# One core, one transformer layer in f32 by split products: w_ffn_out by Strassen's scheme as well

## The chip, the cores and the metric

One core of a Trainium2 chip runs the whole layer. The metric is the device time of one execution in microseconds (us). Five engines work side by side: PE (TensorE, matrix products; PEld is its loading of weights), DVE (VectorE), ACT (ScalarE), POOL (GpSimd) and SP (SyncE, which here only issues transfers).

## The reference

A batch of one, 512 tokens, width 1024, one layer. The first half mixes tokens in four branches (a short convolution, a gated spatial mixing, and two kinds of attention), gates them and multiplies by `w_out`. The second half, in which the change lies, is a gated feed-forward block with 2816 hidden rows:

```
h = h + mixer(rms_norm(h, norm_mix_g))
h = h + swiglu(rms_norm(h, norm_ffn_g), w_ffn_in, w_ffn_out)

def _swiglu(x, w_in, w_out):
    g, u = jnp.split(x @ w_in, 2, axis=-1)
    return (jax.nn.silu(g) * u) @ w_out
```

All inputs and the output are f32.

## The kernel before, in words

Everything is held transposed: features on the 128 partitions, the 512 tokens along the free axis. A matrix of weights is cut into blocks of 128 x 128. So that PE can run its faster f32 form without losing precision, each operand is split in two parts, `hi` (ACT copies it to the rounded type, line 180) and `lo` (DVE subtracts, line 181), and a product is three matmuls: hi hi, hi lo, lo hi (`mm3`, lines 200 to 202, all through line 187). Weights come in chunks of eight blocks, 128 x 1024 f32 or 512 KB, in the order of use (`STREAM`); SP loads a chunk into `raw`, and ACT and DVE split it into `whi` and `wlo`, of which there are three each.

The feed-forward stage has 22 row tiles of hidden rows (each 128). Rows 0 to 3 (`PLAIN`) are computed by `mm3` with 512 columns while the operands for Strassen's scheme are formed. Rows 4 to 21 go in pairs by Strassen's scheme in Winograd's form (`quad_rows`): the tokens are cut into halves of 256, the 1024 inputs into halves of 512, and for a pair of row tiles the gate side and the up side are the other dimension's halves. Seven products (named by their operands 11, s1, s2, 12, s3, 22, s4) take the place of eight; each has 8 blocks x 3 = 24 matmuls of 256 columns (`product`, lines 890 to 892). The four weight blocks of a pair, each 128 x 1024, are loaded by SP (`quad_pair`, line 873) into four pairs of `sraw` tiles; DVE forms their four sums (lines 913, 915, 922, 927), and ACT and DVE split each product's weights. `quad_begin` starts the next pair's first product ahead of the last two of this one. DVE and ACT combine the products (lines 896, 920, 921, 926, 933, 935, 938), and the pair's hidden rows are split at once into `xg` tiles.

`w_ffn_out` is multiplied in three groups of 8, 8 and 6 rows (`GROUPS`): after the rows of a group, `column` computes for each of the eight output tiles the products with the group's hidden rows, 512 columns each, and DVE adds the sum to the residual `h1[d]` (line 962). In the last group the first two columns begin with four of the six rows, and one of them is put into the last pair; each finished tile is sent out.

A planner (Tile) puts every engine's instructions in an order that it works out ahead of time by a simulated timeline, and sets the waits. The order of the program is a priority to it and not a law, except for PE's instructions in the plain rows (`pinned`). A pool of tiles can be closed and its memory used by a later one (`mix.close()`); tiles of one tag share a number of buffers.

Of the kernel before, what the change touches and what calls it, by code (L numbers as in the profile page):

```python
# [29 lines left out]

PLAIN = 4
GROUPS = (8, 8, 6)

PAIRS = 4
# [20 lines left out]
def unit_stream():  # L55

    s = []

    def block(m, col, ks):
        for k in ks:  # L60
            s.append((m, k, col))

    for k in range(KT):
        for nm in ("sbq", "sbk"):
            for b in range(2):
                s.append(("w_in", k, OFF[nm] + b * P))
# [10 lines left out]
    for first, n in hidden_groups():  # L77
        if not first:
            for j in range(PLAIN):
                block("w_ffn_in", j * P, range(KT))  # L80
                block("w_ffn_in", FFN + j * P, range(KT))
        for d, js, _ in out_steps(first, n):
            block("w_ffn_out", d * P, js)
    return s


def out_steps(first, n):


    rows = range(first, first + n)  # L90
    if first + n < FK:
        return [(d, rows, True) for d in range(KT)]
    return [(0, rows[:-2], False), (1, rows[:-2], False), (0, rows[-2:], True), (1, rows[-2:], True)] + \
        [(d, rows, True) for d in range(2, KT)]
# [13 lines left out]
def hidden_groups():  # L108
    first = 0
    for n in GROUPS:  # L110
        yield first, n
        first += n
    assert first == FK


def quad_stream():

    return [(j, half, side) for j in range(PLAIN, FK, 2) for half, side in ((0, 0), (0, 1), (1, 1), (1, 0))]  # L120
# [3 lines left out]
NCHUNK = -(-len(STREAM) // UNITS)  # L124
# [3 lines left out]
def mixer_kernel(ctx, tc, xT, units, quads, wt1, wt2, wsT, small, out):  # L128
# [6 lines left out]
    sm = ctx.enter_context(tc.tile_pool(name="sm", bufs=4))  # L135
    psum = ctx.enter_context(tc.tile_pool(name="psum", bufs=1, space=bass.MemoryType.PSUM))

    mix = ExitStack()
    slots = mix.enter_context(tc.tile_pool(name="slots", bufs=1))

    BUFS = dict(y=18, att=4, aug=6, mrg=8, tmp=6, gt=4)
    KEEP = ("mrg", "tmp", "gt")
# [6 lines left out]
    def slot(tag, dtype=F32):  # L149
        return (keep if tag in KEEP else slots).tile([P, T], dtype, tag=tag, bufs=BUFS[tag], name=nm(tag))  # L150
# [56 lines left out]
    def load_units(c, part, parts):  # L207
        if part == 0:
            chunks[c] = (wpool.tile([P, UNITS * P], F32, tag="raw", bufs=3, name=nm("raw")),
# [32 lines left out]
    sml = const.tile([P, N_SMALL], F32, name="sml")  # L242
# [7 lines left out]
    ssum = slot("mrg")  # L250
# [22 lines left out]
    ident_r = const.tile([P, P], F32R, name="ident_r")  # L273
# [6 lines left out]
    tri = const.tile([P, P], F32, name="tri")  # L280
# [3 lines left out]
    ntri = const.tile([P, P], F32, name="ntri")  # L284
    negs = const.tile([P, P], F32, name="negs")
# [3 lines left out]
    ntri_r = const.tile([P, P], F32R, name="ntri_r")  # L289
    V.tensor_copy(ntri_r, ntri)  # L290
    negs_r = const.tile([P, P], F32R, name="negs_r")
# [5 lines left out]
    mask_sb = const.tile([P, P], F32R, name="mask_sb")  # L297
# [4 lines left out]
    mask_fx = const.tile([P, P], F32R, name="mask_fx")  # L302
# [8 lines left out]
    hm_r = const.tile([P, P], F32R, name="hm_r")  # L311
# [41 lines left out]
    nc.sync.dma_start(out=sml, in_=small)  # L353
    rc, r1 = rms(ssum, "r1")
# [12 lines left out]
    u = []  # L367
    for b in range(2):
        t = slot("mrg")
# [4 lines left out]
    def token_group(wt, width, nk, banks):  # L374

        for c in range(KT // nk):
            raw = wpool.tile([P, nk * width], F32, tag="raw", bufs=3, name=nm("raw"))
# [59 lines left out]
    gq = const.tile([P, 1], F32, name="gq")  # L437
# [283 lines left out]
    def gates(n):  # L721
        gate = {}
        for kind, d in gate_steps(n):
# [9 lines left out]
            if n == 0:  # L733
                merged[d] = slot("mrg")
# [14 lines left out]
    h1, hg = [], []  # L749
    hsum = slot("tmp")  # L750
    tab = const.tile([P, 1], F32, name="tab")
    for d in range(KT):
# [5 lines left out]
        hd = slot("mrg")  # L758
        V.tensor_tensor(hd, ps, x_d, op=ALU.add)
        g = sml[:, C_G2 + d:C_G2 + d + 1]  # L760
# [14 lines left out]

    mix.close()
    ffn = ctx.enter_context(tc.tile_pool(name="ffn", bufs=1, reuse_waits="tile"))
    H = T // 2

# [3 lines left out]
    def plain_product(row, col, ks, ps):  # L783
        for k in ks:
            mm3(ps, next_unit(("w_ffn_in", k, col)), hg[k], k == 0, k == KT - 1)

    def plain_gate(ps):
        t = slot("gt")
# [5 lines left out]
    def plain_up(j, t):  # L794
        up = bank("g") if j else up0
        plain_product(j, FFN + j * P, range(0 if j else 2, KT), up)
# [10 lines left out]
    plain_product(0, 0, range(6), gp)  # L807
    _, r2 = rms(hsum, "r2", lambda: (plain_product(0, 0, range(6, KT), gp), plain_product(0, FFN, range(2), up0)))
# [9 lines left out]

    A = [ffn.tile([P, 2, 4, H], F32, tag="sraw", bufs=PAIRS, name=nm("A")) for _ in range(2)]

    def normed(half):
        for k in range(4):
            d = 4 * half + k
            g = sml[:, C_G2 + d:C_G2 + d + 1]
            V.scalar_tensor_tensor(A[half][:, :, k], h1[d].rearrange("p (h t) -> p h t", h=2), g,
                                   r2.rearrange("p (h t) -> p h t", h=2), op0=ALU.mult, op1=ALU.mult)

    def operand(src):
        hi, lo = (ffn.tile([P, 4, H], F32R, tag="op", bufs=14, name=nm("op")) for _ in range(2))
        split(hi, lo, src)  # L830
        return hi, lo

    a11, a21, a12, a22 = A[0][:, 0], A[0][:, 1], A[1][:, 0], A[1][:, 1]
    X = {}

    def operands(step):
        if step == 0:
            normed(0)
            X["11"] = operand(a11)
        elif step == 1:  # L840
            normed(1)
            X["22"] = operand(a22)
            V.tensor_tensor(a22, a21, a22, op=ALU.subtract)
            X["s1"] = operand(a22)
        elif step == 2:
            V.tensor_tensor(a21, a11, a21, op=ALU.subtract)
            V.tensor_tensor(a11, a22, a11, op=ALU.subtract)
            X["s2"] = operand(a11)
            X["12"] = operand(a12)
        elif step == 3:  # L850
            X["s3"] = operand(a21)
            V.tensor_tensor(a12, a12, a11, op=ALU.add)
            X["s4"] = operand(a12)

    t = plain_gate(gp)
    for j in range(PLAIN):
        if j:
            gp = bank("g")
            plain_product(j, j * P, range(KT), gp)
            t = plain_gate(gp)  # L860
        if j < 4:
            operands(j)
        plain_up(j, t)
    for j in range(PLAIN, 4):
        operands(j)
    pinned[0] = False

    QUADS = quad_stream()

    def quad_pair(c):  # L870
        raw = ffn.tile([P, 2, UNITS * P], F32, tag="sraw", bufs=PAIRS, name=nm("sraw"))
        for i in range(2):
            nc.sync.dma_start(out=raw[:, i], in_=quads[c + i])
        return raw[:, 0], raw[:, 1]

    def quad_parts(src):
        hi = wpool.tile([P, UNITS * P], F32R, tag="whi", name=nm("whi"))
        lo = wpool.tile([P, UNITS * P], F32R, tag="wlo", bufs=3, name=nm("wlo"))
        split(hi, lo, src)
        return hi, lo  # L880

    def product(ps, src, x, first=False):

        (wh, wl), (xh, xl) = quad_parts(src), X[x]
# [9 lines left out]
    def copied(ps):  # L894
        t = slot("tmp")
# [3 lines left out]
    begun = {}  # L899

    def quad_begin(j):
        c = QUADS.index((j, 0, 0))
        b = quad_pair(c) + quad_pair(c + 2)
        px = bank("a")
        product(px, b[0], "11", True)
        begun[j] = b, px, copied(px)

    def quad_rows(j):
        if j not in begun:
            quad_begin(j)  # L910
        (b11, b12, b22, b21), px, p1 = begun.pop(j)
# [7 lines left out]
        gate = [slot("gt"), slot("gt")]  # L919
        V.tensor_tensor(gate[0], py, p1, op=ALU.add)  # L920
        S.activation(gate[0], gate[0], AF.Silu)
        V.tensor_tensor(b11, b12, b11, op=ALU.subtract)
        product(px, b11, "s3")
# [3 lines left out]
        V.tensor_tensor(b21, b12, b21, op=ALU.add)  # L927
        if j + 2 < FK:
            quad_begin(j + 2)
        else:  # L930
            column(*steps.pop(0))
        product(px, b21, "22")
        S.activation(gate[1], px, AF.Silu)
        product(pz, b22, "s4")
        V.tensor_tensor(early, pz, u, op=ALU.subtract)
        hi, lo = (two().rearrange("p j (h t) -> p j h t", h=2) for _ in range(2))
        for half, up in ((1, late), (0, early)):
            V.tensor_tensor(up, up, gate[half], op=ALU.mult)
# [96 lines left out]
```

## Time and profile before

| | us |
|---|---|
| median of 3 runs | 793.16 (792.85 to 793.42) |
| the profiled execution | 792.95 |
| its span, first to last instruction | 791.2 |
| PE, PEld, DVE, ACT, POOL busy | 785.9, 677.7, 546.5, 367.8, 8.4 |

A time in the profile counts from the span's start. The feed-forward stage takes the span from about 440 us on. Busy times are unions of the shown pieces; a matmul's shown length holds its way through the array, and the next one starts before it ends, so that the distance of starts is what it costs. DVE's operations overlap a little in the same way.

### The profile page before, as it was taken

The page shows a single profiled execution, that of the slowest core. Times are in us where ns is not written, and L with a number is a line of the kernel's source. Part 1 is how long each engine was busy: PE and PEld are TensorE (multiplying, and loading weights), DVE is VectorE, ACT ScalarE, POOL GpSimd, SP SyncE. Part 2 cuts the span into 40 slices and gives each one's busy share as a digit, 9 for nine tenths or more (in the row PEclk, how much of TensorE's full clock was granted, in tenths as well). Part 3 has the DMA queues.
Part 4 walks back from the last instruction along what each step waited for, and adds up shares of the span by engine and source line. Part 5 has one row for each costly group of instructions (what it writes and reads, how often), then busy time and mean ns, then how long its engine had stood idle before and what let it go on. Part 6 is the DMA issues. An engine that isn't in the chain of part 4 may idle for free.

```text
span 791.2 us, 10770 instructions
## 1 busy us (share of the span) xinstructions
PE 785.9 (99%) x4319; PEld 677.7 (86%) x4319; DVE 546.5 (69%) x780; ACT 367.8 (46%) x522; POOL 8.4 (1%) x23
## 2 busy tenths in 40 slices
PE   9999999999999999999999999999999999999998
PEld 6888888888888888888888888998899998899987
DVE  8447886877677688756665698873478874468752
ACT  7336427677743455434343554552155552135530
POOL 1000000000000000000000000000000000000000
PEclk9999999999999999999999999999999999999999
DMA  7423222222123222222243343352133333211021
GB/s 286 133 80 104 97 80 81 80 81 74 59 80 106 81 81 81 80 93 81 106 161 119 131 155 115 108 184 82 54 107 109 107 119 121 80 54 54 28 94 67
DMA packets 24098, 78.98 MB, mean 100 GB/s; under 512 B 2672, under 2 KB 2928, under 8 KB 24048
## 3 DMA queue, kind: packets, MB, share of 16 engines
q1 hardware_dynamic: 22608, 75.80, 28.4%
q10 hardware_dynamic: 1440, 2.49, 1.0%
q8 instruction: 34, 0.56, 0.3%
q14 instruction: 16, 0.13, 0.1%
HBM read 76.18 MB, written 2.10 MB: 99 GB/s over the span
## 4 chain that ended last, share of the span: by engine, by line
PE 97%; ACT 1%; DVE 0%; DMA 0%; issue 0%; SPq 0%
PE ps L187 65%; PE ps L891 8%; PE ps L892 8%; PE ps L890 7%; PE ps L198 1%; PE ps L196 1%; PE ps L197 1%; PE ps L535 1%; PE ps L701 1%; DMA raw<-units 0%; PE ps L685 0%; PE ps L601 0%; PE ps L568 0%; PE ps L600 0%; PE ps L686 0%; PE ps L569 0%
## 5 line engine op out<-in xcount | busy, mean ns | idle before, releaser
L187 PE MATMUL ps<-xg,whi 128*128 128x512 f32 (+1 forms) x1212 | 377.8, 393 | 0.5 <-DVE xg L181 0.3
L187 PEld LDWEIGHTS ps<-xg,whi 128*128 128x128 f32 x1212 | 226.2, 188 | 50.3 <-DVE xg L181 0.8
L187 PE MATMUL ps<-xg,wlo 128*128 128x512 f32 (+1 forms) x606 | 235.8, 393 | 0.0
L180 ACT ACTIVATE whi<-raw 128x1024 fp32r<-128x1024 f32 (+2 forms) x104 | 106.4, 1025 | 180.1 <-PE ps L187 135.7
L181 DVE TENSOR_TENSOR wlo<-raw,whi 128x1024 fp32r<-128x1024 f32 (+2 forms) x104 | 122.8, 1182 | 49.7 <-ACT whi L180 49.4
L891 PE MATMUL ps<-op,whi 128*128 128x256 f32 x504 | 141.0, 281 | 0.0
L890 PE MATMUL ps<-op,whi 128*128 128x256 f32 x504 | 140.6, 280 | 0.0
L892 PE MATMUL ps<-op,wlo 128*128 128x256 f32 x504 | 139.2, 281 | 0.0
L187 PEld LDWEIGHTS ps<-xg,wlo 128*128 128x128 f32 x606 | 113.9, 188 | 24.9
L180 ACT ACTIVATE whi<-sraw 128x1024 fp32r<-128x1024 f32 x63 | 66.9, 1062 | 97.3 <-PE ps L187 32.7
L890 PEld LDWEIGHTS ps<-op,whi 128*128 128x128 f32 x504 | 95.3, 189 | 0.2
L891 PEld LDWEIGHTS ps<-op,whi 128*128 128x128 f32 x504 | 94.7, 188 | 0.2
L892 PEld LDWEIGHTS ps<-op,wlo 128*128 128x128 f32 x504 | 93.9, 188 | 0.0
L181 DVE TENSOR_TENSOR wlo<-sraw,whi 128x1024 fp32r<-128x1024 f32 x63 | 77.1, 1224 | 23.1 <-ACT whi L180 22.9
L187 PE MATMUL ps<-y,whi 128*128 128x512 f32 x224 | 70.5, 394 | 0.0
L962 DVE TENSOR_TENSOR mrg<-ps,mrg 128x512 f32<-128x512 f32 (+1 forms) x25 | 16.7, 669 | 64.5 <-PE ps L187 64.5
L187 PEld LDWEIGHTS ps<-y,whi 128*128 128x128 f32 x224 | 42.0, 188 | 9.7
L187 PE MATMUL ps<-y,wlo 128*128 128x512 f32 x112 | 44.2, 394 | 0.0
L727 ACT ACTIVATE gt<-gt 128x512 f32<-128x512 f32 x32 | 20.1, 627 | 23.7 <-DVE gt L726 23.4
L726 DVE TENSOR_TENSOR gt<-ps,r 128x512 f32<-128x512 f32 x32 | 22.0, 687 | 11.3 <-PE ps L187 11.2
L187 PEld LDWEIGHTS ps<-y,wlo 128*128 128x128 f32 x112 | 21.0, 188 | 4.8
L737 DVE SCALAR_TENSOR_TENSOR gt<-gt,ps 128x512 f32<-128x512 f32 x24 | 16.4, 685 | 10.1 <-PE ps L187 6.7
(247 smaller groups left out, 827.7 us busy)
## 6 DMA issues: line engine op xcount, KB each, us to landing
raw<-units SPq DMA_DIRECT2D x90, 512.0 KB, 3.4
sraw<-quads SPq DMA_DIRECT2D x36, 512.0 KB, 4.5
x<-xT SPq DMA_DIRECT2D x8, 256.5 KB, 5.2
raw<-units SPq DMA_DIRECT2D x8, 256.0 KB, 5.2
raw<-wt SPq DMA_DIRECT2D x4, 512.0 KB, 3.9
tmp<-xT ACTq DMA_DIRECT2D x8, 256.0 KB, 3.6
outT<-mrg SPq DMA_DIRECT2D x7, 256.0 KB, 2.0
raw<-wt SPq DMA_DIRECT2D x2, 520.0 KB, 3.3
```

The costliest lines, as they stand in the source:

```text
L180: S.activation(dst_hi, src, AF.Copy)
L181: V.tensor_tensor(dst_lo, src, f(dst_hi), op=ALU.subtract)
L187: i = PE.matmul(**args)
L196: PE.matmul(out=ps, lhsT=ah, rhs=bh, start=start, stop=False)
L197: PE.matmul(out=ps, lhsT=al, rhs=bh, start=False, stop=False)
L726: V.tensor_tensor(t, proj_block(OFF["gate"] + n * D + d * P), r1, op=ALU.mult)
L727: S.activation(t, t, AF.Tanh, scale=0.5)
L737: V.scalar_tensor_tensor(t, t, 1.0, ps, op0=ALU.add, op1=ALU.mult)
L890: PE.matmul(out=dst, lhsT=wh[:, u], rhs=xh[:, k], start=first and k == 0 and jj == 0, stop=False, skip_group_check=True)
L891: PE.matmul(out=dst, lhsT=wh[:, u], rhs=xl[:, k], start=False, stop=False, skip_group_check=True)
L892: PE.matmul(out=dst, lhsT=wl[:, u], rhs=xh[:, k], start=False, stop=ends, skip_group_check=True)
L962: V.tensor_tensor(h1[d][:, cs], src, h1[d][:, cs], op=ALU.add)
```

## The change

`w_ffn_out` is multiplied by Strassen's scheme too for the first 16 of its 22 rows, in two groups of 8: the 8 hidden rows are the inner dimension (halves of 4), a group of four output tiles is the other, and the tokens' halves are as before. A superblock is now either ("in", j), a pair of hidden rows, or ("out", first, half), four output tiles for one group of rows; `superblocks()` lists them: in 4, in 6, in 8, in 10, in 12, out (0, 0), in 14, out (0, 1), in 16, in 18, in 20, out (8, 0), out (8, 1). Then the last 6 rows' columns follow as before with 512 columns. Hidden rows are kept in f32 in tiles of four rows (`quarter`), without a split. A group's seven split operands are formed by eleven steps, which `form()` takes one at a time at four places of each superblock; in the superblock out (8, 0) it takes three steps that split the last six rows.

The first sum of the weights (T1 = B11 + B12) is no longer made by DVE: SP loads B12, and then GpSimd issues a second transfer, which adds B11 from DRAM into the tile (`accum_op`). All weight blocks of this stage now pass through six `sraw` tiles. The mixer's pools hold more of the constants and the chunk tiles, and are closed ahead of the feed-forward stage; residual tiles are allocated in pairs (`row_pair`).

```diff
-PLAIN = 4
-GROUPS = (8, 8, 6)
-PAIRS = 4
+PLAIN = 4
+GROUP = 8
+REST = 16
+BLOCKS = 6
...
+def superblocks():
+    s = [("in", j) for j in range(PLAIN, GROUP, 2)]
+    for first in range(GROUP, FK, GROUP):
+        rows = [("in", j) for j in range(first, min(first + GROUP, FK), 2)]
+        outs = [("out", first - GROUP, half) for half in range(2)]
+        s += rows[:3] + outs[:1] + rows[3:] + outs[1:]
+    return s
...
+    rawp = mix.enter_context(tc.tile_pool(name="rawp", bufs=3))
...
+    opool = ctx.enter_context(tc.tile_pool(name="opool", bufs=1, reuse_waits="tile"))
     ffn = ctx.enter_context(tc.tile_pool(name="ffn", bufs=1, reuse_waits="tile"))
...
+    def block(src, add=None):
+        t = ffn.tile([P, UNITS * P], F32, tag="sraw", bufs=BLOCKS, name=nm("sraw"))
+        nc.sync.dma_start(out=t, in_=src)
+        if add is not None:
+            G.dma_start(out=t, in_=add, accum_op=ALU.add)
+        return t
...
-        V.tensor_tensor(t, up, t, op=ALU.mult)
-        a = two() if j == PLAIN - 1 else ffn.tile([P, 2, T], F32R, tag="plain", bufs=PLAIN - 1, name=nm("plain"))
-        hidden[j] = (a[:, 0], a[:, 1])
-        split(*hidden[j], t)
+        V.tensor_tensor(hidden_rows(j, 1)[:, :, 0], by_half(up), by_half(t), op=ALU.mult)
...
+    def group_tile(name):
+        if name in ("11", "s1", "s2"):
+            return ffn.tile([P, 4, H], F32R, tag="hop", bufs=6, name=nm("hop"))
+        return two().rearrange("p j (h t) -> p (j h) t", h=2)
...
+        return [lambda: operand("11", a11), lambda: operand("22", a22),
+                lambda: differ(a21, a22, a22), lambda: operand("s1", a22),
+                lambda: differ(a11, a21, a21), lambda: differ(a22, a11, a11), lambda: operand("s2", a11),
+                lambda: operand("12", a12), lambda: operand("s3", a21),
+                lambda: V.tensor_tensor(a12, a12, a11, op=ALU.add), lambda: operand("s4", a12)]
...
+    def form():
+        if forming:
+            forming.pop(0)()
...
+    def begin(i):
+        c = 4 * i
+        b = block(quads[c]), block(quads[c + 1], quads[c]), block(quads[c + 2]), block(quads[c + 3])
+        px = bank("a")
+        product(px, b[0], tokens_of(i)["11"], True)
+        begun[i] = b, px, copied(px)
+
+    def superblock(i):
+        if i not in begun:
+            begin(i)
+        (b11, t1, b22, b21), px, p1 = begun.pop(i)
+        X, inner = tokens_of(i), SUPER[i][0] == "in"
         pz, py = bank("a"), bank("a")
-        V.tensor_tensor(b12, b11, b12, op=ALU.add)
-        product(pz, b12, "s1", True)
-        V.tensor_tensor(b12, b12, b22, op=ALU.add)
-        product(px, b12, "s2")
...
+        product(pz, t1, X["s1"], True)
+        form()
+        V.tensor_tensor(t1, t1, b22, op=ALU.add)
+        product(px, t1, X["s2"])
         u = copied(px)
-        product(py, b21, "12", True)
+        product(py, b21, X["12"], True)
+        if inner:
+            gate = [ftile("gt"), ftile("gt")]
+            V.tensor_tensor(gate[0], py, p1, op=ALU.add)
+            S.activation(gate[0], gate[0], AF.Silu)
+        else:
+            V.tensor_tensor(h(0, 0), by_row(py), h(0, 0), op=ALU.add)
+            V.tensor_tensor(h(0, 0), by_row(p1), h(0, 0), op=ALU.add)
+        form()
+        V.tensor_tensor(b11, t1, b11, op=ALU.subtract)
+        product(px, b11, X["s3"])
         v = copied(px)
-        late, early = slot("gt"), slot("gt")
+        late = ftile("gt")
         V.tensor_tensor(late, pz, v, op=ALU.subtract)
+        if not inner:
+            V.tensor_tensor(h(1, 1), by_row(late), h(1, 1), op=ALU.add)
+        V.tensor_tensor(b21, t1, b21, op=ALU.add)
+        if i + 1 < len(SUPER):
+            begin(i + 1)
+        product(px, b21, X["22"])
+        if inner:
+            S.activation(gate[1], px, AF.Silu)
         else:
-            column(*steps.pop(0))
+            V.tensor_tensor(h(0, 1), by_row(px), h(0, 1), op=ALU.add)
+        form()
+        product(pz, b22, X["s4"])
+        early = ftile("gt")
         V.tensor_tensor(early, pz, u, op=ALU.subtract)
+        if inner:
+            rows = hidden_rows(SUPER[i][1], 2)
+            for half, up in ((1, late), (0, early)):
+                V.tensor_tensor(rows[:, half], by_row(up), by_row(gate[half]), op=ALU.mult)
+        else:
+            V.tensor_tensor(h(1, 0), by_row(early), h(1, 0), op=ALU.add)
+        form()
```

## Rows read from the trace of the kernel before

**Rows 1.** The page: busy time of each engine, and PE's granted clock in 40 slices
```profile
PE 785.9 (99%) x4319; PEld 677.7 (86%) x4319; DVE 546.5 (69%) x780; ACT 367.8 (46%) x522; POOL 8.4 (1%) x23
PEclk9999999999999999999999999999999999999999
```
**Rows 2.** PE's waits: for whom, us in total, times, longest
```profile
PE ps L239 <- DVE one L234: 1.3, 1, 1.3
...
PE ps L187 <- DVE xg L181: 0.3, 1, 0.3
PE ps L187 <- ACT whi L180: 0.2, 1, 0.2
```
**Rows 3.** Chain that ended last, from 500 us: start, us, what
```profile
...
528.90 44.54 PE ps L187 x192
...
652.87 44.49 PE ps L187 x192
...
763.45 24.71 PE ps L187 x123
788.18 0.42 DVE mrg L962
```
**Rows 4.** Timeline of PE at the ends of columns and pairs: start, us, what
```profile
528.74 0.63 PE L187 MATMUL ps<-plain,whi 128*128 128x512 f32 x2
...
573.05 0.40 PE L187 MATMUL ps<-xg,wlo 128*128 128x512 f32 x1
573.28 0.28 PE L890 MATMUL ps<-op,whi 128*128 128x256 f32 x1
...
652.71 0.63 PE L187 MATMUL ps<-xg,whi 128*128 128x512 f32 x2
```
**Rows 5.** Timeline of PE ahead of the last columns; in brackets idle time and releaser
```profile
763.45 0.51 PE L187 MATMUL ps<-xg,whi 128*128 128x512 f32 x1 [0.35 <-DVE xg L181]
```
**Rows 6.** Stretch, us, then busy PE, PEld, DVE, ACT, POOL; clock, transfers' share, GB/s
```profile
449.50:480.30 30.80, 30.80 (x134) 25.01 (x134) 30.79 (x36) 16.02 (x19) 0.00 (x0) 1.00 0.45 154
...
584.93:604.75 19.82, 19.82 (x170) 19.82 (x169) 17.35 (x19) 11.04 (x14) 0.00 (x0) 1.00 0.30 107
604.75:624.57 19.82, 19.82 (x170) 19.82 (x169) 17.63 (x19) 11.08 (x14) 0.00 (x0) 1.00 0.32 107
624.57:644.40 19.83, 19.83 (x170) 19.83 (x169) 17.03 (x18) 11.05 (x14) 0.00 (x0) 1.00 0.31 107
```
**Rows 7.** Timeline of DVE in one row pair
```profile
585.27 1.23 DVE L913 TENSOR_TENSOR sraw<-sraw 128x1024 f32<-128x1024 f32 x1 [1.03 <-DMA sraw<-quads]
586.41 1.22 DVE L181 TENSOR_TENSOR wlo<-sraw,whi 128x1024 fp32r<-128x1024 f32 x1
587.55 0.68 DVE L926 TENSOR_TENSOR gt<-ps,tmp 128x512 f32<-128x512 f32 x1
588.72 1.23 DVE L181 TENSOR_TENSOR wlo<-sraw,whi 128x1024 fp32r<-128x1024 f32 x1 [0.49 <-ACT whi L180]
...
594.02 0.69 DVE L181 TENSOR_TENSOR xg<-gt,xg 128x512 fp32r<-128x512 f32 x1
594.62 0.69 DVE L935 TENSOR_TENSOR gt<-ps,tmp 128x512 f32<-128x512 f32 x1
```
**Rows 8.** The page: issues of 512 KB: issuer, count, KB each, median us to landing
```profile
raw<-units SPq DMA_DIRECT2D x90, 512.0 KB, 3.4
sraw<-quads SPq DMA_DIRECT2D x36, 512.0 KB, 4.5
```
**Rows 9.** Timeline of ACT in the same row pair
```profile
585.03 1.06 ACT L180 ACTIVATE whi<-sraw 128x1024 fp32r<-128x1024 f32 x1 [1.52 <-PE ps L891]
...
587.63 1.06 ACT L180 ACTIVATE whi<-sraw 128x1024 fp32r<-128x1024 f32 x1 [1.05 <-PE ps L891]
```
**Rows 10.** The Strassen blocks' loads
```profile
DMA to landing us min/median/max: 3.4/4.5/8.0
```
**Rows 11.** Chain that ended last, where the attention's last products stand
```profile
354.15 1.00 PE ps L535 x7
```

More of the change, by code (lines that the diff above doesn't have):

```diff
@@ L76, in unit_stream, with ffn_stream @@
         block("w_out", d * P, range(KT))
[L77 to L83, printed above, removed]
-    return s
[L87 to L94, printed above, removed]
+    return s
+def ffn_stream():
+    s = [("w_ffn_in", k, side * FFN + j * P) for j in range(PLAIN) for side in range(2) for k in range(KT)]
+    return s + [("w_ffn_out", j, d * P) for d in range(KT) for j in range(REST, FK)]
 def gate_steps(n):
@@ L105, in gate_steps, with unit_of, mixer_kernel @@
             yield "branch", d - late
[L108 to L120, printed above, removed]
+def superblocks():
[5 more added lines that the diff above has]
+    return s
+def unit_of(block, half, side, jj, k):
+    if block[0] == "in":
+        return "w_ffn_in", 4 * half + k, side * FFN + (block[1] + jj) * P
+    return "w_ffn_out", block[1] + 4 * half + k, (4 * block[2] + 2 * side + jj) * P
 STREAM = unit_stream()
-NCHUNK = -(-len(STREAM) // UNITS)
+FFN_STREAM = ffn_stream()
+SUPER = superblocks()
 @with_exitstack
-def mixer_kernel(ctx, tc, xT, units, quads, wt1, wt2, wsT, small, out):
+def mixer_kernel(ctx, tc, xT, units, ffn_units, quads, wt1, wt2, wsT, small, out):
     nc = tc.nc
@@ L149, in slot, with row_pair @@
     def slot(tag, dtype=F32):
-        return (keep if tag in KEEP else slots).tile([P, T], dtype, tag=tag, bufs=BUFS[tag], name=nm(tag))
+        return slots.tile([P, T], dtype, tag=tag, bufs=BUFS[tag], name=nm(tag))
+    def row_pair():
+        return keep.tile([P, 2, T], F32, tag="mrg", bufs=4, name=nm("mrg"))
     def two(dtype=F32R):
@@ L208, in load_units @@
         if part == 0:
-            chunks[c] = (wpool.tile([P, UNITS * P], F32, tag="raw", bufs=3, name=nm("raw")),
+            chunks[c] = (rawp.tile([P, UNITS * P], F32, tag="raw", name=nm("raw")),
                          wpool.tile([P, UNITS * P], F32R, tag="whi", name=nm("whi")),
@@ L823, in normed @@
             d = 4 * half + k
[L824 to L853, printed above, removed]
+            V.scalar_tensor_tensor(A[half][:, :, k], by_half(h1[d]), g2[:, d:d + 1], by_half(r2), op0=ALU.mult, op1=ALU.mult)
@@ new lines, in op_tile, with operands, operand, differ @@
+    def op_tile(name):
+        return opool.tile([P, 4, H], F32R, tag="op", bufs=14, name=nm("op"))
+    def group_tile(name):
+        if name in ("11", "s1", "s2"):
+            return ffn.tile([P, 4, H], F32R, tag="hop", bufs=6, name=nm("hop"))
+        return two().rearrange("p j (h t) -> p (j h) t", h=2)
+    def operands(X, first, last, tile_of):
+        a11, a21, a12, a22 = first[:, 0], first[:, 1], last[:, 0], last[:, 1]
+        def operand(name, src):
+            X[name] = tile_of(name), tile_of(name)
+            split(*X[name], src)
+        def differ(a, b, to):
+            V.tensor_tensor(to, a, b, op=ALU.subtract)
+        return [lambda: operand("11", a11), lambda: operand("22", a22),
[3 more added lines that the diff above has]
+                lambda: V.tensor_tensor(a12, a12, a11, op=ALU.add), lambda: operand("s4", a12)]
@@ L855, in mixer_kernel @@
+    XIN, XOUT = {}, {}
+    steps = operands(XIN, *A, op_tile)
     t = plain_gate(gp)
@@ L858, in mixer_kernel @@
             gp = bank("g")
-            plain_product(j, j * P, range(KT), gp)
+            plain_product(j * P, range(KT), gp)
             t = plain_gate(gp)
-        if j < 4:
-            operands(j)
+        for i in ((0,), (1, 2, 3), (4, 5, 6, 7), (8, 9, 10))[j]:
+            if i < 2:
+                normed(i)
+            steps[i]()
         plain_up(j, t)
-    for j in range(PLAIN, 4):
-        operands(j)
     pinned[0] = False
[L868 to L880, printed above, removed]
     def product(ps, src, x, first=False):
-        (wh, wl), (xh, xl) = quad_parts(src), X[x]
+        (wh, wl), (xh, xl) = parts(src), x
         for jj in range(2):
@@ L924, in quad_rows @@
         v = copied(px)
-        late, early = slot("gt"), slot("gt")
+        late = ftile("gt")
         V.tensor_tensor(late, pz, v, op=ALU.subtract)
-        V.tensor_tensor(b21, b12, b21, op=ALU.add)
-        if j + 2 < FK:
-            quad_begin(j + 2)
-        else:
-            column(*steps.pop(0))
-        product(px, b21, "22")
-        S.activation(gate[1], px, AF.Silu)
-        product(pz, b22, "s4")
+        if not inner:
+            V.tensor_tensor(h(1, 1), by_row(late), h(1, 1), op=ALU.add)
@@ L937, in quad_rows @@
-        for half, up in ((1, late), (0, early)):
-            V.tensor_tensor(up, up, gate[half], op=ALU.mult)
-            up2 = up.rearrange("p (j t) -> p j t", j=2)
-            split(hi[:, :, half], lo[:, :, half], up2)
-        for jj in range(2):
-            hidden[j + jj] = tuple(t[:, jj].rearrange("p h t -> p (h t)") for t in (hi, lo))
-    def column(d, js, done):
-        last = ks[-1] == FK - 1
-        if d not in banks:
-            banks[d] = bank("g")
-        ps = banks[d]
-        units = [(next_unit(("w_ffn_out", j, d * P)), hidden[j], j == ks[0], j == ks[-1]) for j in js]
-        parts = 2 if last and d == KT - 1 else 1
-        for i in range(parts):
-            cs = slice(i * T // parts, (i + 1) * T // parts)
-            for unit, x, start, stop in units:
-                if parts == 1:
-                    mm3(ps, unit, x, start, stop)
-                else:
-                    mm3(half_banks[i][:, :T // 2], unit, tuple(p[:, cs] for p in x), start, stop)
-            if done:
-                src = ps[:, cs] if parts == 1 else half_banks[i][:, :T // 2]
-                V.tensor_tensor(h1[d][:, cs], src, h1[d][:, cs], op=ALU.add)
-                if last:
-                    (nc.scalar if i else nc.sync).dma_start(out=out[d * P:(d + 1) * P, cs], in_=h1[d][:, cs])
@@ L966, in mixer_kernel @@
-    for first, n in hidden_groups():
-        ks = range(first, first + n)
-        banks, steps = {}, out_steps(first, n)
-        for j in ks[::2]:
-            if j not in hidden:
-                quad_rows(j)
-        half_banks = [bank("a"), bank("a")] if ks[-1] == FK - 1 else None
-        for step in steps:
-            column(*step)
-    assert pos[0] == len(STREAM)
+        if inner:
[4 more added lines that the diff above has]
+            V.tensor_tensor(h(1, 0), by_row(early), h(1, 0), op=ALU.add)
@@ new lines, in superblock, with last_rows @@
+        form()
+    rest = {}
+    def last_rows(j):
+        hi, lo = (op_tile("rest").rearrange("p (j h) t -> p j h t", j=2) for _ in range(2))
+        split(*(t.rearrange("p j h t -> p h j t") for t in (hi, lo)), hidden[j // 4][:, :, j % 4:j % 4 + 2])
+        for jj in range(2):
+            rest[j + jj] = tuple(t[:, jj].rearrange("p h t -> p (h t)") for t in (hi, lo))
+    for i, block_ in enumerate(SUPER):
+        if block_[0] == "in" and block_[1] % GROUP == 0 and block_[1]:
+            first = block_[1] - GROUP
+            XOUT[first] = {}
+            forming += operands(XOUT[first], hidden[first // 4], hidden[first // 4 + 1], group_tile)
+        if block_[0] == "out":
+            assert not forming
+            if ("in", FK - 2) in SUPER[:i] and not rest:
+                forming += [lambda j=j: last_rows(j) for j in range(REST, FK, 2)]
+                rest[REST] = None
+        superblock(i)
@@ new lines, in mixer_kernel @@
+    assert not forming
+    for d in range(KT):
+        ps = bank("g")
+        us = [(ffn_unit(("w_ffn_out", j, d * P)), rest[j], j == REST, j == FK - 1) for j in range(REST, FK)]
+        n = 2 if d == KT - 1 else 1
+        for i in range(n):
+            cs = slice(i * T // n, (i + 1) * T // n)
+            if n == 2:
+                ps = bank("a")[:, :H]
+            for unit, x, start, stop in us:
+                mm3(ps, unit, tuple(p[:, cs] for p in x), start, stop)
+            V.tensor_tensor(h1[d][:, cs], ps, h1[d][:, cs], op=ALU.add)
+            (nc.scalar if i else nc.sync).dma_start(out=out[d * P:(d + 1) * P, cs], in_=h1[d][:, cs])
```

137 lines of the change are left out of this document (81 added, 56 removed).

## The prediction, made before the changed kernel ran

> **What bounds the kernel now.** I read the busy table first: TensorE (PE) is busy for 785.9 of 791.2 us, VectorE (DVE) for 546.5, ScalarE (ACT) for 367.8, and PE's clock is granted in full in every slice [rows 1]. A busy PE row can hide waits, so the second view is PE's waits: four, 2.3 us in all, the longest 1.3 at the start; the one in the feed-forward stage is 0.3 us on `xg` [rows 2]. The third is the chain that ended last: from 500 us on it is PE almost everywhere, with two unbroken pieces of 192 matmuls of line 187, 44.54 and 44.49 us [rows 3]. So time moves here only if PE's work shrinks, or if something begins to hold PE up.
>
> PE's price is read as a pitch, since the shown 0.28 or 0.39 us of one matmul overlap the next. The first w_ffn_out group's columns run from 528.74 to 573.28 us; then, up to 652.71, come 28 Strassen products, that is four row pairs of seven (row 8's first product lies ahead of the stretch, and row 16's in it): 79.43 us [rows 4]. That is 232 ns for a matmul of 512 columns and 79.43 / 672 = 118 ns for one of 256.
>
> **The change: PE.** Removed: the columns of the first two groups, 2 groups x 64 blocks x 3 = 384 matmuls, by the two chain pieces 44.54 + 44.49 = 89.03 us [rows 3]. Added: four superblocks of 7 products x 24 = 672 matmuls of 256 columns with operands of the same shapes as in the four measured pairs, 79.43 us [rows 4]. Net -9.60 us; a bare 7/8 of 89.03 would be -11.1, and 1.5 us of that goes because two matmuls of 256 cost 236 ns against 232. The last 48 blocks, the plain rows and the nine superblocks of w_ffn_in keep their matmuls.
>
> Also removed: the wait at 763.45, 0.35 us [rows 5]. Before, the last pair's hidden rows are split just ahead of the columns that use them. Now two superblocks (40 us) lie between row 20 and those columns, and their splits are formed in the first of them. -0.35 us. The end itself (last sum 0.42 us, then the output's transfer) keeps its form.
>
> **DVE, off the path, but how far?** In three quiet superblocks DVE is busy 17.35, 17.63 and 17.03 us of 19.82, mean 17.34, so it idles 2.48, and PE does not wait [rows 6]. By starts that follow each other at once, an operation of 1024 elements takes 1.14 us of DVE (585.27, 586.41, 587.55) and one of 512 0.60 (594.02, 594.62) [rows 7].
> - w_ffn_in superblock: the sum for T1 goes to the transfer (-1.14) and the two splits of hidden rows go (-1.20): 15.00 us.
> - w_ffn_out superblock: seven operations on 512 (P5 and P1 into h, late and its add, P7, early and its add) where an inner one keeps five: 16.2 us.
> - Forming a group's operands: 11 steps of one DVE operation each at 1.14, in the twelve places of three superblocks (4, 4, 3): 19.56, 19.56 and 18.42 us. Twice.
> - The splits of the last six rows: three steps in one out superblock, 19.62 us.
>
> All are below 19.82, the tightest by 0.2 us. ACT goes from 11.05 us to at most 11.05 - 1.2 + 3 x 1.06 = 13.0. What hides the forming is thus DVE's idle time, nearly all of it. If that cover is gone: a late `wlo` holds the next product, and behind it all of PE. Bounds: 0 below, since work nowhere exceeds PE's (a gain is excluded: these steps shorten nothing on PE). Above, all of the old idle stays as forced waits on ACT, PE or transfers: 2.22 us in each of four superblocks, 1.08 in two, 2.28 in one = 13.3 us. The nearest row is 449.50 to 480.30, in which DVE is busy 30.79 of 30.80 us and PE does not miss anything [rows 6]; there, though, a split weight block lasts PE 24 x 232 ns = 5.6 us, here 2.8. I take 1.0 us, near the lower end.
>
> **T1 by an adding transfer.** Thirteen of 512 KB, issued by GpSimd (POOL), which has nothing else queued in this stage. What waits: POOL for the plain load of the tile, then the split of T1 on ACT and DVE, and behind it product s1. No transfer of before is issued by GpSimd or adds; the blocks' issues are all SP's [rows 8]. The room comes from the six buffers. T1 of superblock i+1 takes the one that the last block (B22) of i-1 leaves after its split, at 586.41 + 1.23 = 587.64 (its `hi` started at 585.03). The `hi` of s1 starts at 587.63 and again one superblock later, 607.45 [rows 7, 9]. So 19.8 us, less a plain load of 4.5 [rows 8], leaves 15.3 for the adding transfer without anything moving. With three `whi` buffers `hi` is made two products (5.7 us) ahead, of which the split takes 1.06 + 1.23: some 3.3 us more, 18.6, until PE waits. The nearest rows are plain loads, 3.4 to 8.0 us, median 4.5; it reads twice as much, so I take twice 4.5, 9 us, bounds 3.4 and 16 (twice the longest) [rows 8, 10]: hidden at both ends, 0 us.
>
> The Trainium skill, page "SBUF — State Buffer", section "SBUF: two separate sides", warns of just this: the descriptors of a transfer issued from GpSimd are written by GpSimd, which is locked out while VectorE runs an operation of a two-port mode, so that the transfer looks blocked by VectorE. Section "Who interferes with whom" says that a tensor_tensor has no such mode, and tensor_tensor is what DVE runs here [rows 7]; no run so far shows such a transfer. By the rule for the locking operations the slower rival below would be the forecast, by the second the sum stays.
>
> SP's queue issues 130 weight blocks as before (94 chunks and 36 blocks then, 64 + 14 chunks and 52 blocks now), and waits for buffers in the order in which they come free. Memory moves (the chunk tiles from an open pool into one laid over the mixer's) cost 0 unless a load has to wait: third rival.
>
> **Sum.** -9.60 - 0.35 + 1.0 = -8.95. The profiled execution took 792.95 us (span 791.2, 1.75 around it), so 784.0; the median of the runs, 793.16, is 0.21 higher, so 784.2.
>
> **Rivals.**
> 1. DVE becomes the bound in the seven superblocks with extra steps. For: 19.56 of 19.82, with an in-order queue, and waits on ACT that it had even at 88% [rows 7]. Against: the saturated 30.8 us without a PE wait [rows 6]; and when DVE is late, ACT and PE have already delivered, so its waits go. Up to +13.3 on 783.0: 796.3; half of it 789.6.
> 2. T1 comes late: slower than before. Place: the `hi` of s1, PE waiting for it. An excess e over 18.6 us is paid once in two superblocks (a tile's buffer is two superblocks old), 6.5 e in all. It eats the 8.95 at e = 1.4, and passes "slower by over 0.2%" at (8.95 + 1.6) / 6.5 = 1.6, that is from transfers of 20.2 us on; at 25 us, 784.2 + 6.5 x 6.4 = 826. For: an operation that no row shows. Against: it must take more than four plain loads.
> 3. The join from w_out to the feed-forward stage opens. If the first chunk's buffer must wait for the mixer's memory, PE waits a load, `hi` and `lo`: 3.4 + 1.06 + 1.23 = 5.7 us, once: 789.9. For: `raw` was in a pool that stays open, and `sraw` is in a new one. Against: by the order of the tags it lies over the attention's tiles, whose last products (line 535) end at 355 us [rows 11], some 90 us before.
> 4. The change does not do what it says, in that products with operands from `hop` and `xg` tiles run at another pitch. Against: 512-column products with operands from `plain` and from `xg` start at the same pitch [rows 4]. At 132 ns for 118 the saving would be gone (672 x 14 ns = 9.4 us): 793.6.
>
> **How the numbers follow.** A change of 0.2% (1.6 us) is about what a measurement of this kernel can tell from none. Forecast 0.66 (own range 782.5 to 786.5). Rival 1 beyond that 0.17, of which 0.03 ends within 0.2% and 0.02 slower. Rival 2 0.06. Rival 3 0.09. Rival 4 0.02. Faster: 0.66 + 0.12 + 0.09 + 0.01 = 0.88; same 0.03 + 0.01 = 0.04; slower 0.02 + 0.06 = 0.08. The range runs from 782.3 (no stall, 783.2, less the spread of the runs and some unseen gain) to 790.0, which takes in rival 3 and half of rival 1's bound, and leaves out about 0.15.
>
> **What would show it.** Right: PE's matmuls 288 more (672 for 384, in records up to the missing ones), 79 to 80 us for the four out superblocks, no PE wait over 0.5 us between 500 us and the end, DVE busy 95% or more in the forming superblocks. Wrong: PE waits on `wlo` that recur in the superblocks of rows 8 to 12 and 16 to 20 (rival 1); ACT or DVE waiting on a transfer into `sraw` with the adding queue's time above 18.6 us (rival 2); one PE gap between 435 and 450 us (rival 3); a pitch other than 118 ns (rival 4). A saving below 7 or above 11 us refutes the forecast's sum.

## The result: slower, 805.74 us against 793.23

The changed kernel takes 805.74 us in the median (803.79 to 806.18), the kernel before 793.23 beside it: ratio 1.0154, 95% interval 1.0136 to 1.0171. The forecast was 784.2 us. The profiled execution took 806.18 us, span 804.5.

The page's busy rows of after (answering to [rows 1]): PE does less work, as planned, but its span share falls from 99 to 97%, and the row of its clock shows an 8 in two slices, those around 452 and 673 us.

```profile
PE 784.0 (97%) x4607; PEld 689.3 (86%) x4607; DVE 584.3 (73%) x811; ACT 391.0 (49%) x541; POOL 19.8 (2%) x36
...
PEclk9999999999999999999999899999999998999999
```

PE's waits of after (for whom, us in total, times, longest). Of [rows 2] the one for `xg` is gone; the rows shown here are new or grown, 15.5 us together, all for split weights or for DVE:

```profile
PE ps L924 <- DVE wlo L182: 5.1, 2, 3.1
PE ps L188 <- ACT whi L181: 5.0, 3, 3.0
PE ps L922 <- ACT whi L181: 3.8, 4, 2.3
...
PE ps L922 <- DVE gt L975: 1.1, 2, 0.9
PE ps L188 <- DVE wlo L182: 0.5, 1, 0.5
```

Where they lie is seen by cutting the Strassen part at the same matmul of every superblock. Windows of after (stretch, us, then busy PE, PEld, DVE, ACT, POOL; clock, transfers' share, GB/s), answering to [rows 6]; the last two stretches together are two superblocks:

```profile
...
547.65:573.87 26.22, 22.27 (x171) 21.45 (x170) 22.86 (x23) 12.41 (x15) 0.86 (x1) 0.93 0.38 103
573.87:593.57 19.70, 19.70 (x171) 19.70 (x170) 14.96 (x15) 10.01 (x12) 0.86 (x1) 1.00 0.51 135
593.57:613.33 19.76, 19.76 (x170) 19.76 (x170) 15.54 (x16) 9.49 (x11) 0.86 (x1) 1.00 0.51 134
...
633.04:657.50 24.46, 24.46 (x209) 24.34 (x209) 21.58 (x22) 15.99 (x19) 0.86 (x1) 1.00 0.49 133
657.50:682.10 24.60, 18.49 (x132) 17.66 (x131) 21.63 (x22) 9.45 (x11) 0.86 (x1) 0.86 0.30 82
```

Quiet superblocks take 19.7 us, w_ffn_out's among them. One stretch takes 26.22, 6.5 too much, of which 3.95 is PE idle (26.22 - 22.27) and the rest PE at the lower clock; the last two together take 49.06, 9.6 too much, of which 6.11 is PE idle (24.60 - 18.49). Between 573.87 and 593.57, where the prediction had forming steps still going on, DVE is busy 14.96 us: all of them are already done. In the chain of waits of after (start, us, what) the long stretch is DVE's, and in it the forming stands in a row with the weights' split (lines 891 and 897 are a group's differences and its sum, `xg` and `hop` its operands):

```profile
550.41 0.93 DVE part L891
551.34 1.14 DVE xg L182
552.48 1.13 DVE wlo L182
...
555.25 1.23 DVE part L897
556.48 1.13 DVE hop L182
...
562.82 1.15 DVE wlo L182
564.01 0.58 PE ps L924
```

Ten of the group's eleven steps run between 537.6 and 561.1 us, a little over one superblock and not three; the other one, the split of operand 11, ran already at 496.1. DVE's timeline of after, the first and the last of the ten:

```profile
537.57 1.22 DVE L182 TENSOR_TENSOR xg<-part,xg 128x1024 fp32r<-128x1024 f32 x1
...
559.86 1.23 DVE L182 TENSOR_TENSOR xg<-part,xg 128x1024 fp32r<-128x1024 f32 x1
```

The planner, to whom program order is only a priority, moved the steps ahead of their places.

The third place is the join of the two halves. PE's timeline of after (start, us, what; in brackets idle time and releaser), and ACT's:

```profile
440.37 0.40 PE L188 MATMUL ps<-y,wlo 128*128 128x512 f32 x1
443.77 0.73 PE L188 MATMUL ps<-xg,whi 128*128 128x512 f32 x2 [3.00 <-ACT whi L181]
445.04 0.80 PE L188 MATMUL ps<-xg,wlo 128*128 128x512 f32 x1 [0.53 <-DVE wlo L182]
445.63 1.05 PE L188 MATMUL ps<-xg,whi 128*128 128x512 f32 x2
446.48 0.63 PE L188 MATMUL ps<-xg,wlo 128*128 128x512 f32 x1
```
```profile
442.16 0.61 ACT L773 ACTIVATE tmp<-mrg 128x512 f32<-128x512 f32 x1
442.68 2.94 ACT L181 ACTIVATE whi<-sraw 128x1024 fp32r<-128x1024 f32 x3
```

The first chunk's load was issued by SP at 410.38 us; no transfer is late. Its split, and two more, stand in ACT's order behind the mixer's last operation. PE idles 3.53 us, and from 445.63 on three matmuls take 1.28 us instead of 0.70, until 450.75: four such triples, 2.3 us more.

6.5 + 9.6 + some 6 = 22 us: that is about the distance from the forecast, 21.5 us.

### The profile page after: what moved, and what is told of

The parts are those of the page before. It is cut to its first block, busy times and chain, and to the rows that moved or that the text cites. A ratio compares the mean times of both kernels' runs of the same rounds, so it can differ in the third digit from the quotient of the medians.

```text
span 804.5 us, 11458 instructions
## 1 busy us (share of the span) xinstructions
PE 784.0 (97%) x4607; PEld 689.3 (86%) x4607; DVE 584.3 (73%) x811; ACT 391.0 (49%) x541; POOL 19.8 (2%) x36
## 4 chain that ended last, share of the span: by engine, by line
PE 93%; DVE 4%; ACT 1%; issue 1%; DMA 0%; SPq 0%; ACTq 0%; DVEq 0%
PE ps L188 54%; PE ps L924 10%; PE ps L923 10%; PE ps L922 10%; PE ps L199 1%; PE ps L197 1%; PE ps L198 1%; PE ps L538 1%; DVE wlo L182 1%; DVE xg L182 1%; PE ps L704 1%; DMA raw<-units 0%; ACT whi L181 0%; DVE part L891 0%; PE ps L688 0%
## 5 line engine op out<-in xcount | busy, mean ns | idle before, releaser
L188 PE MATMUL ps<-xg,whi 128*128 128x512 f32 x896 | 284.1, 397 | 3.9 <-ACT whi L181 3.9
L188 PEld LDWEIGHTS ps<-xg,whi 128*128 128x128 f32 x896 | 168.8, 190 | 41.6 <-ACT whi L181 5.1
L181 ACT ACTIVATE whi<-sraw 128x1024 fp32r<-128x1024 f32 x105 | 110.8, 1060 | 144.9 <-PE ps L923 66.4
L188 PE MATMUL ps<-xg,wlo 128*128 128x512 f32 x448 | 176.3, 399 | 0.5 <-DVE wlo L182 0.5
L182 DVE TENSOR_TENSOR wlo<-sraw,whi 128x1024 fp32r<-128x1024 f32 x105 | 127.9, 1224 | 50.7 <-ACT whi L181 50.5
L181 ACT ACTIVATE whi<-raw 128x1024 fp32r<-128x1024 f32 (+2 forms) x74 | 74.5, 1010 | 97.6 <-PE ps L188 78.8
L182 DVE TENSOR_TENSOR wlo<-raw,whi 128x1024 fp32r<-128x1024 f32 (+2 forms) x74 | 86.1, 1164 | 37.3 <-ACT whi L181 36.7
L922 PE MATMUL ps<-xg,whi 128*128 128x256 f32 x128 | 36.1, 282 | 0.2 <-DVE gt L975 0.2
L923 PE MATMUL ps<-xg,whi 128*128 128x256 f32 x128 | 35.8, 280 | 0.0
L924 PE MATMUL ps<-xg,wlo 128*128 128x256 f32 x128 | 35.7, 279 | 0.0
L188 PE MATMUL ps<-op,whi 128*128 128x512 f32 (+1 forms) x108 | 30.6, 370 | 1.0 <-ACT whi L181 1.0
```

Source lines behind the costliest of these rows:

```text
L181: S.activation(dst_hi, src, AF.Copy)
L182: V.tensor_tensor(dst_lo, src, f(dst_hi), op=ALU.subtract)
L188: i = PE.matmul(**args)
L922: PE.matmul(out=dst, lhsT=wh[:, u], rhs=xh[:, k], start=first and k == 0 and jj == 0, stop=False, skip_group_check=True)
L923: PE.matmul(out=dst, lhsT=wh[:, u], rhs=xl[:, k], start=False, stop=False, skip_group_check=True)
L924: PE.matmul(out=dst, lhsT=wl[:, u], rhs=xh[:, k], start=False, stop=ends, skip_group_check=True)
```

## The experiments

Each was timed in 5 rounds beside the kernel before.

**1. Forming steps kept at their places**

```diff
     def split(dst_hi, dst_lo, src):
-        S.activation(dst_hi, src, AF.Copy)
-        V.tensor_tensor(dst_lo, src, f(dst_hi), op=ALU.subtract)
+        at_place(S.activation(dst_hi, src, AF.Copy))
+        at_place(V.tensor_tensor(dst_lo, src, f(dst_hi), op=ALU.subtract))
...
         if forming:
+            placed[0] = True
             forming.pop(0)()
+            placed[0] = False
```

`at_place` calls `tc.keep_in_program_order` while `placed` is set; the group's differences and the sum go through it too, and so do the last six rows' splits, which `form()` also takes.

> The changed kernel, with its forming steps (ACT and DVE instructions alike) kept at their places in program order, so that the planner can't move a group's eleven steps into one superblock. Theory A (the loss is made of 6.5 and 9.6 us where the planner put each group's steps into one superblock, and of 6.8 us at the join): the two stretches go back to about 19.7 us a superblock, the join stays: 805.7 - 16 = 789 to 791 us. Rival B (the forming superblocks have too much DVE work wherever it stands: rival 1 of the prediction): the same 16 us come back in smaller pieces over six superblocks, 800 us or more. Rival C (the two long stretches come from the adding transfers): nothing changes, 805 us.

Measured: 789.99 us, ratio 0.9963 [0.9949, 0.9977]: 15.75 us less than the changed kernel, by the order of the same instructions alone. B and C fall. The first group's eleven steps now stand between 531.2 and 595.1 us, 64 us (not strictly in the program's order: one split stands behind the difference that follows it). DVE's timeline of this kernel, the last of them:

```profile
593.92 1.22 DVE L188 TENSOR_TENSOR xg<-part,xg 128x1024 fp32r<-128x1024 f32 x1
```

**2. The first two chunks into the mixer's tiles**

```diff
     assert pos[0] == len(STREAM)
+    ahead = []
+    for c in range(2):
+        raw = rawp.tile([P, UNITS * P], F32, tag="raw", name=nm("raw"))
+        nc.sync.dma_start(out=raw, in_=ffn_units[c])
+        ahead.append(parts(raw))
     mix.close()
...
-            fpos[1] = parts(block(ffn_units[c]))
+            fpos[1] = ahead[c] if c < len(ahead) else parts(block(ffn_units[c]))
```

> The changed kernel, with the first two chunks of the feed-forward stage loaded into the mixer's chunk tiles and split ahead of the place where the mixer's pools close; the forming steps are left to the planner. Theory A: the 3.4 us gap behind the last w_out matmul and the slower clock after it go, 6 to 7 us: 798.5 to 800 us, and both long superblocks stay. Rival (the gap is set by the last rows' own sums and splits, not by the weights' place): 804 to 806 us, with the wait now on another line.

Measured: 799.30 us, ratio 1.0076 [1.0064, 1.0089], 6.44 less. For the first chunk no ACT instruction stands between the old and the new place in the program, only the closing of the pools, so it is the tile or that closing that decides, and not the place. (The second chunk's old place stands behind the norm's ACT instruction, the new one ahead of it.) ACT's timeline of this kernel: the two splits now stand among the mixer's work, and PE has no gap there.

```profile
429.71 1.06 ACT L181 ACTIVATE whi<-raw 128x1024 fp32r<-128x1024 f32 x1 [3.42 <-issue]
...
435.28 1.06 ACT L181 ACTIVATE whi<-raw 128x1024 fp32r<-128x1024 f32 x1 [3.37 <-issue]
```

**3. Both edits**

> Both edits: forming steps at their places, and the first two chunks split ahead of the close. Theory A: 805.7 - 16 - 6.5 = 783 us (782 to 785), below both kernels. Under B about 794, under C about 799.

Measured: 785.24 us, ratio 0.9897 [0.9883, 0.991]; the profiled execution took 784.6. This is just above theory A's 782 to 785 and far from B's 794 and C's 799, and it is faster than both kernels. Windows of this kernel (columns as before). The cut is at another matmul, near the start of product 12, so that a stretch holds four products of one superblock and three of the next. The stretches from 594.25 and 633.71 us hold w_ffn_out's four products each; the others are those in which a group is formed, and the one from 693.43 us holds the second group's last three steps and the first of the last rows' splits:

```profile
534.55:554.44 19.89, 19.85 (x170) 19.65 (x168) 17.93 (x19) 11.89 (x15) 0.86 (x1) 1.00 0.45 133
554.44:574.57 20.13, 20.13 (x169) 19.96 (x170) 18.49 (x19) 12.72 (x15) 0.86 (x1) 1.00 0.47 132
574.57:594.25 19.68, 19.68 (x170) 19.68 (x170) 19.09 (x20) 10.84 (x13) 0.86 (x1) 1.00 0.49 135
594.25:613.96 19.71, 19.71 (x170) 19.71 (x170) 17.01 (x18) 8.88 (x10) 0.86 (x1) 1.00 0.51 139
...
633.71:653.44 19.73, 19.73 (x170) 19.73 (x170) 16.67 (x18) 9.73 (x11) 0.86 (x1) 1.00 0.44 130
653.44:673.33 19.89, 19.84 (x169) 19.64 (x169) 17.88 (x19) 11.91 (x15) 0.86 (x1) 1.00 0.48 133
673.33:693.43 20.10, 20.10 (x169) 19.95 (x170) 18.49 (x19) 12.70 (x15) 0.86 (x1) 1.00 0.47 131
693.43:713.99 20.56, 19.95 (x171) 19.75 (x170) 19.72 (x20) 12.72 (x15) 0.86 (x1) 1.00 0.47 130
```

**4. T1 by DVE again**

```diff
-        b = block(quads[c]), block(quads[c + 1], quads[c]), block(quads[c + 2]), block(quads[c + 3])
+        b = block(quads[c]), block(quads[c + 1]), block(quads[c + 2]), block(quads[c + 3])
+        V.tensor_tensor(b[1], b[1], b[0], op=ALU.add)
```

> As the third kernel, but T1 is a sum on DVE again (1.14 us in each of thirteen superblocks) and not an adding transfer. By the prediction's count the forming superblocks then hold 19.56 + 1.14 = 20.7 us of DVE work for 19.7 us of PE, four of them by 1.0 and two of them about even, and the one with the last rows 20.8: if DVE's total decides, 783 + 5 x 1 = 788 us (786 to 790). If the queue lets work slip into the quiet superblocks beside them, under 784.5 us, and the adding transfer is worth nothing here.

Measured: 791.79 us, ratio 0.9981 [0.9973, 0.999], 6.55 above the third (its runs spread from 790.28 to 793.46). DVE does become a limit once it has 1.14 us more in a forming superblock. Windows and a wait of this kernel:

```profile
553.41:573.93 20.52, 20.21 (x168) 19.86 (x169) 18.75 (x19) 11.64 (x14) 0.00 (x0) 1.00 0.31 103
573.93:595.17 21.24, 19.97 (x168) 19.77 (x168) 20.20 (x21) 12.03 (x15) 0.00 (x0) 1.00 0.30 101
```
```profile
PE ps L934 <- DVE wlo L188: 5.9, 8, 1.8
```

It cost more than the 5 us expected: a stretch with DVE at 18.75 of 20.52 us is late too. The chain of waits of this kernel shows why (line 955 is T1's sum): the sum itself waits for a block's load, and DVE, in order, with it.

```profile
562.95 1.24 DVE wlo L188
564.20 4.35 DMA sraw<-quads
568.64 0.53 DVE sraw L955
```

**5. A group's steps in one superblock, placed by hand**

```diff
-        if forming:
+        for _ in range(3 if len(forming) > 0 else 0):
+            if not forming:
+                break
             placed[0] = True
```

> As the third kernel (785.2 us), but a group's eleven forming steps stand at the four places of one superblock (3, 3, 3, 2) and are kept there: the planner has no part in it. Theory A (it is the piling up of DVE work in one superblock that costs): that superblock holds 15.0 + 11 x 1.14 = 27.5 us of DVE for 19.7 us of PE, 7.8 us too much, twice, less what the weight blocks split ahead cover, and with some time at the lower clock: 785.2 + 13 to 18 = 798 to 803 us, with the two stretches as long as in the changed kernel. Rival (the planner's other moves made the long stretches, not the piling up): under 790 us.

Measured: 796.22 us, ratio 1.0038 [1.0026, 1.0051], 11.0 above the third kernel, a little less than expected. Windows:

```profile
540.76:566.87 26.11, 22.72 (x171) 22.32 (x170) 23.93 (x24) 15.02 (x18) 0.86 (x1) 0.87 0.38 102
...
645.73:666.00 20.27, 20.05 (x171) 19.84 (x170) 18.62 (x19) 12.22 (x14) 0.86 (x1) 1.00 0.46 126
666.00:691.00 25.00, 21.64 (x170) 21.23 (x170) 23.80 (x23) 13.83 (x17) 0.86 (x1) 0.93 0.40 110
```

The first stretch is as long as the changed kernel's, 26.11 against 26.22: piling up, without the planner's hand in it, is enough for a loss of that size. The second group costs 5.9 us here (0.57 + 5.3) and 9.6 there; the 3.7 us between them, which go with where the planner put that group, remain unexplained.

**6. Two steps at each place** (as the fifth, with 2 for 3)

> As the third kernel, but two forming steps at each place: eight in a group's first superblock, three in its second. DVE holds 15.0 + 8 x 1.14 = 24.1 us in the first and 18.4 in the second, for 19.7 us of PE in each. If DVE's lateness is paid where it arises: 4.4 us a group, 785.2 + 9 = 794 us. If it is carried into the next superblocks and worked off there in their idle 1.3 and 4.7 us, behind weight blocks that are split ahead: under 788 us.

Measured: 789.77 us, ratio 0.9957 [0.9943, 0.9971], 4.5 above the third: between the two. Windows: the first group pays where it stands, the second hardly at all.

```profile
540.05:564.26 24.21, 21.36 (x170) 21.15 (x170) 23.10 (x24) 14.56 (x17) 0.86 (x1) 0.93 0.38 110
564.26:583.96 19.70, 19.70 (x171) 19.70 (x170) 15.78 (x16) 10.01 (x12) 0.86 (x1) 1.00 0.48 135
...
663.40:683.51 20.11, 20.01 (x170) 19.81 (x170) 20.08 (x21) 12.21 (x14) 0.86 (x1) 1.00 0.40 106
```

For the first group the lateness was paid in the same superblock; the room of the next one (15.78 us of DVE work) came too late. The second group's stretch holds three DVE operations and 3 us of DVE work less than the first's (21 against 24, 20.08 against 23.10); why the planner's order differs there isn't known.

**7. No adding transfers**

```diff
-        b = block(quads[c]), block(quads[c + 1], quads[c]), block(quads[c + 2]), block(quads[c + 3])
+        b = block(quads[c]), block(quads[c + 1]), block(quads[c + 2]), block(quads[c + 3])
```

> As the third kernel, but without the adding transfers: T1 is the block B12 alone, so B11's part of T1 is left out of the result. If the transfers lie wholly off the path, as the prediction had it: 784.8 to 785.6 us, no change. If they make the tiles of T1 late for their splits or slow the other loads: 783.5 us or less, with the small waits of the forming superblocks gone.

Measured: 784.66 us, ratio 0.9893 [0.988, 0.9907] beside the third kernel's 0.9897 [0.9883, 0.991]: no difference that can be told. The transfers lie off the path, as far as this measurement can tell.

**8. The last rows' splits over two superblocks**

```diff
-                forming += [lambda j=j: last_rows(j) for j in range(REST, FK, 2)]
+                wait_ = [lambda: None]
+                forming += [x for j in range(REST, FK, 2) for x in wait_ + [lambda j=j: last_rows(j)]]
```

> As the third kernel, but the three splits of the last rows, which stood at three places of one superblock of w_ffn_out (19.72 us of DVE work in a stretch of 20.56), stand at two places of it and one of the next. By the idle time of DVE: the stretch goes back to 19.75, 784.4 us. If the 0.6 us wait there comes from the order within the superblock and not from its sum: 785.2 us.

Measured: 784.13 us, ratio 0.9884 [0.9871, 0.9898], 1.1 below the third; the two intervals overlap, so the trace has to show it. Window, cut at the same matmuls as the third kernel's 20.56: the stretch is whole again, with DVE at 18.80 for 19.72.

```profile
693.34:713.02 19.68, 19.68 (x171) 19.68 (x170) 18.80 (x20) 11.78 (x14) 0.86 (x1) 1.00 0.50 136
```

**9. PE in program order to the end** (the products' matmuls through `mm`, with `pinned` set)

> As the eighth kernel (784.1 us), with PE's matmuls too kept in program order from the first Strassen product to the end, so that the last 48 blocks' columns don't start amid the last two products, where PE waits 1.0 us for a split of a weight block. If that wait comes from the interleaving: 783.1 us. If ACT's order sets it (the block's split stands behind the last products' splits either way): 784.1 us, the wait at another place.

Measured: 784.11 us, ratio 0.9882 [0.9865, 0.9898], as the eighth. The wait moved, from the block's `whi` to ACT's copy of a product. ACT makes that split first and the copy behind it in both kernels (at 738.42 and 739.39 us in the eighth, 738.66 and 739.63 here), so ACT's order sets it. PE's waits of this kernel:

```profile
PE ps L192 <- ACT tmp L938: 1.5, 1, 1.5
```

**10. One chunk ahead instead of two** (`range(1)` in the second edit, on the eighth kernel)

> As the eighth kernel (784.1 us), with one chunk instead of two loaded and split ahead of the close. If the whole price of the join is the first chunk's split on ACT (442.7 to 443.7 us, behind the mixer's last work there), one is enough, since the second chunk is wanted 5.6 us later: 784.1 us. If every chunk in a tile of the new pools comes late, and one only moves the gap by a chunk: a gap again, of 1 us or more, at 446 us, 785.5 us or more.

Measured: 785.40 us, ratio 0.9899 [0.9884, 0.9914], 1.3 above the eighth, with a gap of 0.54 us where 1 or more was expected. In the two traces 0.7 us of the difference lies in PE's first matmuls, before 20 us of the span, and has nothing to do with the join; some 0.9 us is the join's. ACT's and PE's timelines: the second chunk's split, in a tile of the new pool, stands behind all of the mixer's ACT work and behind the norm's (line 328).

```profile
445.75 0.26 ACT L328 ACTIVATE rc<-ps,eps 128x4 f32<-128x4 f32 x1 [2.98 <-PE ps L192]
445.92 2.94 ACT L187 ACTIVATE whi<-sraw 128x1024 fp32r<-128x1024 f32 x3
```
```profile
448.28 0.51 PE L192 MATMUL ps<-xg,wlo 128*128 128x512 f32 x1 [0.54 <-DVE wlo L188]
```

So the first chunk was not the whole price. But the norm's instruction stands ahead of the second chunk's split in the program too, so this run doesn't tell whether every such tile is put in late or only the first. Why the planner puts them there, when their loads were issued 30 us before, no run shows; that its timeline lets a new pool begin only when the closed ones are done is a guess.

## Why the prediction was wrong, step by step

- **PE's term held.** -9.60 forecast. The two stretches of the third kernel with most of w_ffn_out's products take 19.71 and 19.73 us, and nothing disturbs them; four are 78.9 instead of 79.43, so -10.1. The other quiet superblocks also take 19.7 where [rows 6] had 19.82; that was not foreseen and is not explained.
- **"11 steps ... in the twelve places of three superblocks (4, 4, 3)" failed.** This step cost 15.75 us more than the price of its work, for which 1.0 was taken. The sum of DVE's work was right, and its price was near: with the steps where the text put them (third kernel) the five tight stretches exceed 19.72 by 0.17, 0.41, 0.17, 0.38 and 0.84, 2.0 us. What was wrong is that they would stand there. The program order is a priority to the planner, and only PE's plain rows were pinned: the group's last step, which the first experiment holds at 593.9 us, ran at 559.9. The saturated stretch [rows 6] that spoke for a low price may not have been a parallel either, as the prediction itself said (there a weight block lasts PE 5.6 us, here 2.8); no run tests that.
- **"Memory moves ... cost 0 unless a load has to wait" failed.** 6.44 us by the second experiment. Rival 3 named the place, and by luck nearly the price (5.7), but not the mechanism: no load waited, the split was put in late on ACT, and 2.3 us are PE at the lower clock.
- **The -0.35 at 763.45 [rows 5] was not gained.** That wait went, but a block's `whi` is late there instead, 1.1 us in the third kernel and still 1.0 in the eighth: ACT's order at the end, by the ninth.
- **T1 was right.** No PE wait leads to it, and without the addition the time stays. Issues of after (issuer, count, KB, median us to landing) against [rows 8]: 5.4 us, where 9 were taken.

```profile
sraw<-quads SPq DMA_DIRECT2D x52, 512.0 KB, 3.4
...
sraw<-quads POOLq DMA_DIRECT2D x13, 512.0 KB, 5.4
```

  The fear of the locked-out GpSimd did not come true: by the Trainium skill, page "SBUF — State Buffer", section "Who interferes with whom", tensor_tensor has no 2-port mode, though with both inputs in SBUF it contends with GpSimd's reads. The trace agrees with the first: the transfer issued at 557.4 us, while DVE ran tensor_tensor after tensor_tensor, took 5.2 us, against the median of 5.4.
- **Rival 1** had the right engine and the wrong reason: the work of the forming superblocks fits, if only just (the fourth experiment shows the edge). **Rival 4** is refuted by the 19.7 us.

Taken one by one, the two failed steps are worth 15.75 + 6.44 = 22.2 us; both edits together give back 20.5 (805.74 to 785.24). Where the 1.7 us between them lie no run shows. With both put right, the mechanism that was priced gives 785.24 as the third kernel, 1.0 above the forecast, and 784.13 as the eighth, 1.2% below the kernel before.

## What to carry to other kernels

A balance of an engine's work per stretch holds only if the work runs in that stretch: where a planner may move it, ask for each hidden step from when its inputs are ready, and either price it there or keep it at its place. When a pool is closed between two stages, let the first inputs of the next stage pass through tiles of the old one. Adding blocks by a transfer is a good way to relieve a vector engine that is close to its limit: here it was worth 6.6 us (fourth against third), part of it because DVE's own sum also waited for a load, and it had no cost that could be measured.

## What the hardware showed beside this

After the gap of 3.0 us at the join PE's granted clock fell: 0.67 in the mean from 443.77 to 445.57 us, then 0.50 (1.2 of 2.4 GHz) up to 450, under unbroken matmuls, at 0.43 us a matmul for 0.23. Windows of after (columns as before):

```profile
443.77:445.57 1.80, 1.27 (x3) 0.80 (x4) 1.80 (x2) 1.80 (x2) 0.00 (x0) 0.67 0.00 0
445.57:450.00 4.43, 4.43 (x12) 3.40 (x11) 1.68 (x2) 0.04 (x1) 0.00 (x0) 0.50 0.82 263
```

Shorter waits did not all leave it alone. The gap of 0.54 us in the tenth kernel left the clock at 1.00, and so did one of 1.3 us in the fourth (up to 595.17 us). One of 1.8 us in the fourth (up to 718.11 us) was followed by 0.50 from 719.09 to 722.50 us.
